# The last store of a row-wise maximum-norm kernel, cut into two halves on two queues

## Chip, cores and metric

The kernel runs on one NeuronCore of one Trainium2 chip. The metric is the device time of one execution in microseconds (us), lower being better. Before the change three runs took 626.57, 627.03 and 627.04 us; the median is 627.03 us.

## What is computed

The input is an 8192 x 8192 matrix of float32, 268.44 MB. For each row the largest absolute value is wanted, so the output is 8192 float32 numbers, 32 KB.

```python
def setup_inputs():
    return {"x": np.random.randn(8192, 8192).astype(np.float32)}

def reference(x):
    return np.linalg.norm(x, ord=np.inf, axis=1)
```

## The kernel before

Each of the 128 partitions takes whole rows. The rows are divided in two groups. The first 6144 rows, the bulk, are loaded by 24 DMAs (line 303), each bringing two rows, that is 16384 numbers, to every partition; one VectorE instruction per load (`absmax`, line 296) reduces both rows and writes two results into `r_bulk`. The last 2048 rows, the tail, are 16 rows per partition. They are loaded in smaller and smaller pieces (lines 315 and 341, 20 and 12 DMAs), so that VectorE has little left to reduce when the last piece arrives. Partial maxima go to `part` and to spare columns of `t`, and the 16 results of each partition end up in `r_tail`, a tile of 128 x 16. All 56 loads are issued by SyncE (SP), in program order, on its own queue.

Two stores write the output. ScalarE (ACT), which computes nothing here, issues the store of `r_bulk` on its queue (line 357): 128 partitions x 4 pieces of 48 bytes, 24 KB. It is held back until the third last reduction has run. SP issues the store of `r_tail` (line 359): 128 partitions x 64 bytes, 8 KB, contiguous in the output. It needs the last two reductions, one for each of the two rows that end last.

A DMA raises a semaphore when it has landed, by one for each of the 16 DMA engines. The tile framework deals eight such semaphores, called DMAHW0 to DMAHW7, to the DMAs in turn, and it makes a DMA wait for the previous user of its semaphore. The store of `r_bulk` has DMAHW0 (number 100 in the trace), the store of `r_tail` DMAHW1 (101). VectorE counts its finished reductions on semaphore 102.

The end of the program is written by hand in `finish_on_pool` (lines 89 to 140). After the body every engine reports at a barrier (semaphore 96) that GpSimd (POOL) collects and releases (97). Then POOL alone has to see that the stores have landed, and to set the semaphores back to zero for the next execution. The function finds the last DMA of SP and calls its semaphore the lane; it sorts the waits that are still open into the lane's own and the others, and builds this sequence for POOL:

```python
    last = [s for s in waits if s.id == lane]
    others = [s for s in waits if s.id != lane]
...
    tail = [wait([s], []) for s in others]
    for a, b in ((lo, lane - 1), (lane + 1, hi)):
        if a <= b:
            tail.append(clear_range(nc, clear, a, b))
...
    tail.append(wait(last, [reset]))
```

So POOL waits for the other stores, clears all semaphores below the lane, clears all above it, and last waits for the lane and subtracts its count. In the kernel before the lane is DMAHW1 and the others are DMAHW0 alone, so the end of POOL's program is: wait for the store of `r_bulk`, clear 99 to 100, clear 102 to 108, wait for the store of `r_tail` and reset 101.

`drop_implied_waits` (line 152) removes waits of SP's DMAs that another wait already implies; it does not touch DMAs of ACT. The remaining functions at the end of the kernel move the first load and a clearing instruction forward and take VectorE out of the opening barrier.

In the built program all 58 DMAs, loads and stores, move 128 partitions, and the builder has put the mark `ant_dge_precooked: true` on each of them.

Of the kernel before, what the change touches and what calls it, by code (L numbers as in the profile page):

```python
# [38 lines left out]
def segments(loads, cols):  # L39

    out, at = [], 0
    for i, w in enumerate(loads):
        end = at + w
        while at < end:
            r = at // cols
            to = min(end, (r + 1) * cols)
            out.append((i, r, at - r * cols, to - at))
            at = to
    return out
# [201 lines left out]
@with_exitstack  # L251
def kernel(
    ctx: ExitStack,
    tc: tile.TileContext,
    x: bass.AP,
    out: bass.AP,
    G: int = 6,
    B: int = 2,
    BUFS: int = 3,
    PAD: int = 256,  # L260
    LINE: int = 128,
):
    nc = tc.nc
    P = nc.NUM_PARTITIONS
    rows, cols = x.shape
    W = B * cols


    n_tail = B * (len(TAIL) + 1)
    n_bulk_rows = rows // P - n_tail  # L270
    assert n_bulk_rows % (G * B) == 0
    A = n_bulk_rows // (G * B)
    split = n_bulk_rows * P
    x_b = x[:split].rearrange("(a p n b) c -> a n p (b c)", p=P, a=A, n=G, b=B)
    out_b = out[:split].rearrange("(a p n b) -> p a (n b)", p=P, a=A, n=G, b=B)
    x_t = x[split:].rearrange("(p t b) c -> t p (b c)", p=P, b=B)
    out_t = out[split:].rearrange("(p t) -> p t", p=P)

    outp = ctx.enter_context(tc.tile_pool(name="outp", bufs=1))
    sbuf = ctx.enter_context(tc.tile_pool(name="sbuf", bufs=BUFS))  # L280

    segs = [segments(loads, cols) for loads in TAIL]
    k_max = max(sum(r == b for _, r, _, _ in s) for s in segs for b in range(B))
    parts_of = [sum(r == b for r, _ in LAST) - 1 for b in range(B)]
    assert sum(parts_of) <= PAD

    r_bulk = outp.tile([P, A, G * B], F32)
    r_tail = outp.tile([P, n_tail], F32)
    part = outp.tile([P, n_tail - B, k_max], F32)
    used = [HEAD, A * G * B, n_tail, (n_tail - B) * k_max]  # L290
    gap = -sum(-(-n // STEP) * STEP for n in used) % LINE
    outp.tile([P, gap], F32, name="gap")
    nc.gpsimd.memset(part[:], 0.0)  # L293

    def absmax(o, i):
        return nc.vector.reduce_max(  # L296
            out=o, in_=i, axis=X, apply_absolute_value=True
        )

    for a in range(A):  # L300
        for n in range(G):
            t = sbuf.tile([P, W + PAD], F32, tag="t")
            nc.sync.dma_start(out=t[:, :W], in_=x_b[a, n])
            absmax(
                r_bulk[:, a, n * B : (n + 1) * B],
                t[:, :W].rearrange("p (b c) -> p b c", b=B),
            )

    for i, loads in enumerate(TAIL):
        t = sbuf.tile([P, W + PAD], F32, tag="t")  # L310
        todo = segs[i]
        seen = [0] * B
        at = 0
        for j, w in enumerate(loads):
            nc.sync.dma_start(out=t[:, at : at + w], in_=x_t[i][:, at : at + w])
            at += w
            for _, b, c, n in [s for s in todo if s[0] == j]:
                k, lo = seen[b], b * cols + c
                absmax(part[:, i * B + b, k : k + 1], t[:, lo : lo + n])
                seen[b] += 1  # L320

    def after(ins, first, kind):
        info = mybir.DependencyInfo(kind, mybir.DependencyReason.SCHED_ONLY)
        tc.add_manual_dep(ins.ins, first.ins.name, info, reason="order")


    t = sbuf.tile([P, W + PAD], F32, tag="t")
    left = parts_of[:]
    col = [0] * B
    at, slot = 0, {}  # L330
    ends = [w for _, w in LAST[-B:]]
    lo = W - sum(ends)
    for b in range(B):
        slot[b] = -(-lo // LINE) * LINE + ends[b]
        lo = slot[b] + parts_of[b]
    assert lo <= W + PAD
    for j, (b, w) in enumerate(LAST):
        final = left[b] == 0
        to = slot[b] - w if final else at
        frm = b * cols + col[b]  # L340
        nc.sync.dma_start(out=t[:, to : to + w], in_=x_t[len(TAIL)][:, frm : frm + w])
        col[b] += w
        if final:
            r = n_tail - B + b
            absmax(r_tail[:, r : r + 1], t[:, to : slot[b] + parts_of[b]])
        else:
            left[b] -= 1
            k = slot[b] + left[b]
            done = absmax(t[:, k : k + 1], t[:, to : to + w])
            at += w  # L350
        if j == 0:

            ins = absmax(r_tail[:, : n_tail - B], part[:])
            after(ins, done, mybir.DependencyClass.NoSync)
        if j == len(LAST) - 3:

            ins = nc.scalar.dma_start(out=out_b, in_=r_bulk[:])
            after(ins, done, mybir.DependencyClass.Sync)
    nc.sync.dma_start(out=out_t, in_=r_tail[:])
    nc.at_finalize(clear_partials_early)  # L360
    nc.at_finalize(drop_implied_waits)
    nc.at_finalize(start_first_load_early)
    nc.at_finalize(finish_on_pool)
    nc.at_finalize(open_without_vector)
# [30 lines left out]
```

## Time and profile before

| what | value | where it is read |
|---|---|---|
| median of three runs | 627.03 us | the runs |
| span of the profiled execution, first to last instruction | 624.1 us (624.05) | head of the page |
| VectorE busy | 552.4 us, 89% of the span | part 1 |
| DMA traffic | 268.47 MB, mean 430 GB/s | part 2 |
| packets of the load queue q1 | 8064 in the span, 99.7% of 16 engines' time | part 3 |

The page gives no total for the profiled execution besides its span. What lies around the span is 627.03 - 624.05 = 2.98 us if that execution took as long as the median.

The span ends with the last instruction of the program, but the last store is still under way then. The trace also records the semaphores being raised, and it goes on after the span. Its events around the end, in us from the span's start, are these; duration is that of the instruction.

| us | event |
|---|---|
| 621.57 | VectorE's count that releases the store of `r_bulk` |
| 621.59 | ACT issues the store of `r_bulk`, 0.409 |
| 622.04 | ACT's drain before the barrier, 0.153 |
| 622.54 to 623.13 | 512 data packets and 16 semaphore packets of that store on the DMA engines |
| 623.275 to 624.000 | its 16 landings (semaphore 100) |
| 623.297 | VectorE's last count, which releases the store of `r_tail` |
| 623.314 | SP issues the store of `r_tail`, 0.348 |
| 623.720 | SP's drain, 0.123; SP is the last at the barrier, 623.845 |
| 623.947 | POOL's release of the barrier; seen on semaphore 97 at 623.972 |
| 624.065 | POOL clears 99 and 100 |
| 624.138 to 624.166 | POOL clears 102 to 108 |
| 624.157 to 624.37 | 128 data packets and 16 semaphore packets of the store of `r_tail` |
| 624.565 to 624.730 | its 16 landings (semaphore 101) |
| 624.780 | POOL's reset of 101, its last act in the program |
| 624.29, 624.32, then 625.33 to 625.62 | counts on semaphore 2, the runtime's own, after the program |
| 625.52 to 626.22 | the runtime clears all other semaphores |
| 626.45 to 626.80 | a last round of counts on semaphore 2 |

### The profile page before, as it was taken

How to read it: one execution, taken by the hardware profiler on the slowest of the kernel's cores; microseconds unless marked ns; L12 is line 12 of the kernel's file. 1: busy time of each engine (PE TensorE's matmuls, PEld its weight loads, DVE VectorE, ACT ScalarE, POOL GpSimd, SP SyncE). 2: the span in 40 equal slices, each digit the busy share in tenths (PEclk: the TensorE clock that was granted, in tenths of full speed). 3: DMA queues.
4: the chain of work that ended last, by engine and by line, in shares of the span. 5: the costliest groups of instructions: out<-in, count | busy, mean ns of one | idle time of the engine just before them, and what ended most of it. 6: DMA issues, size and time to landing. Idle time of an engine off the chain costs nothing.

```text
span 624.1 us, 151 instructions
## 1 busy us (share of the span) xinstructions
DVE 552.4 (89%) x63; POOL 0.3 (0%) x5
## 2 busy tenths in 40 slices
DVE  0688988889988899888898888988889999999999
POOL 0000000000000000000000000000000000000000
DMA  9999999999999999999999999999999999999998
GB/s 403 470 403 454 420 428 445 403 470 403 470 403 441 433 403 470 403 470 403 470 403 470 403 462 412 437 437 403 470 434 397 440 448 422 422 437 430 429 427 354
DMA packets 8593, 268.47 MB, mean 430 GB/s; under 512 B 1424, under 2 KB 1424, under 8 KB 2832
## 3 DMA queue, kind: packets, MB, share of 16 engines
q1 hardware_dynamic: 8064, 268.44, 99.7%
q10 hardware_dynamic: 528, 0.02, 0.1%
q14 instruction: 1, 0.01, 0.0%
HBM read 268.44 MB, written 0.03 MB: 430 GB/s over the span
## 4 chain that ended last, share of the span: by engine, by line
DMA 63%; DVE 36%; another core or an unknown queue 0%; DVEq 0%; issue 0%
DMA t<-in_x_dram 63%; DVE r_bulk L296 25%; DVE part L296 8%; DVE t L296 3%; DVEq L390 0%; DVE r_tail L296 0%
## 5 line engine op out<-in xcount | busy, mean ns | idle before, releaser
L296 DVE TENSOR_REDUCE r_bulk<-t 128x2 f32<-128x16384 f32 x24 | 413.3, 17220 | 70.6 <-DMA t<-in_x_dram 70.6
L296 DVE TENSOR_REDUCE part<-t 128x1 f32<-128x8192 f32 (+19 forms) x26 | 121.3, 4741 | 0.3
L296 DVE TENSOR_REDUCE t<-t 128x1 f32<-128x1792 f32 (+7 forms) x10 | 16.3, 1692 | 0.0
L296 DVE TENSOR_REDUCE r_tail<-t 128x1 f32<-128x772 f32 (+1 forms) x2 | 1.8, 948 | 0.0
L296 DVE TENSOR_REDUCE r_tail<-part 128x14 f32<-128x42 f32 x1 | 0.2, 192 | 0.0
L293 POOL MEMSET part<- 128x42 f32 x1 | 0.1, 133 | 0.0
L379 POOL MEMSET const-bfloat16-1.0<- 128x1 bf16 x1 | 0.1, 101 | 0.0
L379 POOL MEMSET const-uint8-127<- 128x1 uint8 x1 | 0.1, 101 | 0.0
L379 POOL MEMSET const-float32-0.0<- 128x1 f32 x1 | 0.1, 98 | 0.2 <-issue 0.2
L379 POOL MEMSET const-float32-1.0<- 128x1 f32 x1 | 0.1, 98 | 0.0
## 6 DMA issues: line engine op xcount, KB each, us to landing
t<-in_x_dram SPq DMA_DIRECT2D x2, 4672.0 KB, 37.5
t<-in_x_dram SPq DMA_DIRECT2D x2, 3520.0 KB, 36.2
t<-in_x_dram SPq DMA_DIRECT2D x1, 6336.0 KB, 36.3
t<-in_x_dram SPq DMA_DIRECT2D x1, 5696.0 KB, 40.5
t<-in_x_dram SPq DMA_DIRECT2D x2, 1792.0 KB, 34.3
t<-in_x_dram SPq DMA_DIRECT2D x1, 3392.0 KB, 37.5
t<-in_x_dram SPq DMA_DIRECT2D x1, 3008.0 KB, 44.2
t<-in_x_dram SPq DMA_DIRECT2D x1, 2496.0 KB, 27.3
```

The lines of the kernel that those rows point to most:

```text
L293: nc.gpsimd.memset(part[:], 0.0)
L296: return nc.vector.reduce_max(out=o, in_=i, axis=X, apply_absolute_value=True)
L379: nc = _bacc.Bacc("TRN2", target_bir_lowering=False, num_devices=1)
```

## The change

The store of `r_tail` is replaced by two stores of 64 partitions each. ACT issues the one of partitions 64 to 127, SP the one of partitions 0 to 63. The destination of each is a contiguous 4 KB of the output.

```diff
             ins = nc.scalar.dma_start(out=out_b, in_=r_bulk[:])
             after(ins, done, mybir.DependencyClass.Sync)
-    nc.sync.dma_start(out=out_t, in_=r_tail[:])
+    half = P // 2
+    nc.scalar.dma_start(out=out_t[half:], in_=r_tail[half:, :])
+    nc.sync.dma_start(out=out_t[:half], in_=r_tail[:half, :])
     nc.at_finalize(clear_partials_early)
     nc.at_finalize(drop_implied_waits)
```

`finish_on_pool` is unchanged, but it is given one store more. In the built program ACT's half takes DMAHW1 and SP's half DMAHW2 (103 in the trace), so that the lane is now DMAHW2 and the others are DMAHW0 and DMAHW1. ACT's program gets two instructions: a wait for the load that used DMAHW1 before, and the DMA, which waits for VectorE's last count. The instructions of the other engines are the same up to the end block, where POOL has one wait more. Neither half carries the mark `ant_dge_precooked`.

```
POOL, end block, before                   after
                                          wait DMAHW1 >= 128   (ACT's half)
clear 99..100   [wait DMAHW0 >= 128]      clear 99..102   [wait DMAHW0 >= 128]
clear 102..108                            clear 104..108
wait DMAHW1 >= 128, subtract 128          wait DMAHW2 >= 128, subtract 128
```

## The prediction, made before the changed kernel was run

> **What bounds the kernel now.** I read the page's head first, then the chain of waits, then the last microseconds by timeline, DMA view and SP's waits. The head and the chain's summary say where the 624 us are:
>
> ```profile
> span 624.1 us, 151 instructions
> DVE 552.4 (89%) x63; POOL 0.3 (0%) x5
> DMA 63%; DVE 36%; another core or an unknown queue 0%; DVEq 0%; issue 0%
> ```
>
> The chain consists of loads and of the reductions that follow them, and the change touches neither: all loads stay in SP's queue ahead of the store, with their waits, their tiles and their order. So I take 621 of the 624 us as fixed, and only what follows the last reduction is in play. The last pieces of the chain of waits (start, length, what):
>
> ```profile
> 607.80 13.50 DVE t L296 x9
> 621.30 0.17 issue
> 621.47 0.76 DVE r_tail L296
> 622.24 0.09 issue
> 622.32 0.96 DVEq L390
> ```
>
> The chain ends with VectorE at 623.28. The timeline from 619 us on shows what is issued after it:
>
> ```profile
> 621.47 1.81 DVE L296 TENSOR_REDUCE r_tail<-t 128x1 f32<-128x772 f32 x2
> 621.59 0.41 ACTq L357 DMA_DIRECT2D out_dram<-r_bulk  x1
> 623.31 0.35 SPq L359 DMA_DIRECT2D out_dram<-r_tail  x1
> ```
>
> ACT issues the bulk store 1.72 us before SP issues the last one, and is then free: its drain is over at 622.19. In SP's own waits the last store waits on VectorE and on nothing else, so SP is not a bottleneck there:
>
> ```profile
> SPq L359 <- DVE r_tail L296: 11.6, 1, 11.6
> ```
>
> The DMA view of the stretch 620 to 626 us (40 slices of 0.15 us, tenths busy) shows both stores, and the issue rows give the time from issue to last landing:
>
> ```profile
> DMA  9999999999310000187500000001400000000000
> q10 hardware_dynamic: 528, 0.02, 5.6%
> out_dram<-r_bulk ACTq DMA_DIRECT2D x1, 24.0 KB, 2.4
> out_dram<-r_tail SPq DMA_DIRECT2D x1, 8.0 KB, 1.4
> ```
>
> What the reader is to see: the last store occupies the engines for little more than one slice (the "14"), yet needs 1.4 us. By the events listed with the profile, 0.843 us pass from issue to the first packet (623.314 to 624.157), about 0.21 us are packets (to 624.37), and the last landing comes at 624.730. Data movement is the smallest share, and it is the only one that halving can shrink. POOL closes the program at 624.780, 0.050 us after that landing: the store is on the path that sets the program's end, while POOL's two clears (624.065 to 624.166) are over 0.4 us earlier and cost nothing.
>
> **The change, part by part.**
>
> *Fewer packets per store.* Each half has 64 data packets of 64 bytes instead of 128, four per DMA engine instead of eight; successive packets of one engine stand about 10 ns apart, so a half is over 4 x 10 ns = 0.04 us sooner. But both halves share the 16 engines. If they arrive together the second gains nothing. So -0.04 us for a half that runs alone, 0 if they collide; I take -0.04. The Trainium skill, in "DMA: Bandwidth & Descriptors", section "Issuing engines are not separate DMA queues", says that DMAs of several engines run on the same 16 DMA engines and that issuing them from several only saves the sequencer's time. By that rule the gain here would be 0 rather than 0.04, as no second issue is saved; the sum moves by 0.04 us.
>
> *The issue itself.* Every issue in this trace is of a marked DMA: the loads' take 0.327 to 0.433 us, the last store 0.348, the four-piece bulk store with 512 packets 0.409. The number of packets hardly matters: (0.409 - 0.348)/384 is 0.16 ns for each, so 64 fewer save 0.01 us, and I exclude a larger gain. The halves carry no mark, and no row has an unmarked issue. If the mark means preparation at build time, then the sequencer does that work now, at the worst place, because nothing follows VectorE's last count except the store. Low end: no change, 0.348. High end: the issue grows to the whole 0.843 us that now pass from issue to first packet, +0.50. No row is nearer to one end, so I take the middle, +0.25 (an issue of 0.60 us), for each half. Packets and landing move with it. SP's half: last landing 624.73 + 0.25 - 0.04 = 624.94.
>
> *ACT's half.* It waits for DMAHW1 of a load finished before 616 us, at no cost, and then for VectorE's last count, like SP. ACT has nothing behind the DMA but its drain. Its start reaction is the same (0.021 us after the count for the bulk store, 0.017 for SP's). From its issue to its first packet the bulk store took 622.540 - 621.589 = 0.951 us against SP's 0.843, so ACT's way is 0.11 us longer (0.06 of it the longer issue, which its four-piece shape may explain). I take +0.08, ends 0.05 and 0.11. ACT's half therefore lands at 624.94 + 0.08 = 625.02.
>
> *The barrier.* SP reaches it at 623.845 today, ACT at 622.20. With the longer issue SP comes at 624.09, and ACT, with 0.05 us more for its drain (0.153 plus 0.04 gap), at about 624.2. The release moves from 623.97 to 624.3, still 0.7 us before the landings, which hide it.
>
> *POOL's end.* Here work loses its cover. POOL now waits for ACT's landing first, then clears twice, then waits for SP's half. So the two clears, which today run under the flight of the store, stand behind a landing. From rows of the same instructions: wait satisfied to its end 0.05 (624.730 to 624.780), next the first clear 0.093 (from the release's count at 623.972 to 624.065), the second clear 0.073 after it and 0.028 long, the last wait's reset another 0.05: 0.29 us after ACT's landing. Before it was 0.05. So +0.24 if ACT's half lands last or together with SP's; if it lands more than 0.24 us before SP's it costs nothing. I take it whole, as ACT's is the later one.
>
> *Sum.* 625.02 + 0.29 = 625.31 for POOL's last act, against 624.78: +0.53 us (0.25 issue, 0.08 ACT's way, 0.24 clears, -0.04 packets). Lowest by these bounds: no longer issue, +0.05 for ACT: 0 + 0.05 + 0.24 - 0.04 = +0.25. Highest: 0.50 + 0.11 + 0.24 + 0 = +0.85. The span itself, which ends at the last instruction with a record, should grow as well.
>
> From program to time: POOL's last act is at 624.78, the runtime's last recorded count at 626.80, and I let the 2.02 us between stay. The profiled execution's total is not given; span 624.05 plus 2.98 us around it is the median, 627.03. So I forecast **627.03 + 0.53 = 627.56, rounded 627.6 us**. A measurement of this kernel tells about 0.2% from no change, 1.25 us: the forecast is slower by 0.08% and counts as no change.
>
> **The rivals.**
>
> *The halves are issued one after the other (chance 0.17).* Then the change does not do what it says. Both are released by one count, and SP reacts 4 ns sooner, so ACT's would be second, by one issue more: 0.35 to 0.60 us. It carries POOL's clears along: 625.31 + 0.35 to 0.60 gives +0.88 to +1.13 us, 627.9 to 628.2. For it: nothing in the trace excludes it. Against it: nothing shows it either, as ACT's one issue at 621.59 meets no issue of SP, whose last load was issued by 611.7 (573.31 plus 38.40 in SP's timeline). The Trainium skill, in "Perfetto Trace Analysis", section "DMA Instruction — HWDGE (DVE, Sync)", describes one descriptor generator that sequencers lock for exclusive use, with the lock's wait inside the profiled issue; by that rule the second issue would be the longer record. No run here shows it yet.
>
> *ACT's half lands as slowly as the bulk store did (0.15): slower.* ACT's queue has one sample, 2.41 us from issue to last landing against SP's 1.42. If this belongs to the queue and not to the 512 packets of 48 bytes, ACT's half lands at 623.32 + 2.41 = 625.73, with the longer issue 625.98, and POOL ends 0.29 later, 626.27: +1.49 us, 628.5. It counts as slower once ACT's landing comes later than 624.78 + 1.25 - 0.29 = 625.74, that is 2.42 us after the issue. Against it: of the 2.41 us, 0.59 are packets, and the landings trail the last packet by 0.87 us where the 64-byte store has 0.36; both go with the many small writes.
>
> *The end is covered (0.14).* The runtime's counts come at 624.29 and 624.32, and then not before 625.33, 0.55 us after POOL's reset. If these wait for something other than POOL, say another engine that starts its closing code when the barrier is released, only the barrier's delay of 0.3 us or less is felt: 627.0 to 627.3.
>
> *The gain arrives (0.06).* The issue is no longer, ACT's half lands 0.24 us or more before SP's, and a half is 0.04 us sooner: 627.0, at best 626.9. A gain over 1.25 us is not to be had, since the whole way from VectorE's last count to POOL's reset is 624.78 - 623.30 = 1.48 us and holds an issue, a start and a landing in any case.
>
> **How the numbers follow.** My forecast holds 0.48. Of it 0.06 may run over 1.25 us, if the longer issue exceeds its bound or the runtime's closing round is delayed too. Slower: 0.15 + 0.06 + 0.05 (the worst of the issues in turn with an issue of 0.84 us) = 0.26. Faster: only by scatter of the runs, 0.02. Same: 0.72. The range goes from 627.0 (covered end) to 628.6 (the slow landing, 0.1 above its value).
>
> **What would show it.** Right: the issue record of each half is about 0.6 us instead of 0.35; both start within 0.02 us of VectorE's last count; ACT's landings end about 0.1 us after SP's; POOL's clears stand behind ACT's last landing and its reset of 103 comes near 625.3; everything up to 623.3 is as before. Wrong: one issue record nearly twice as long as the other (in turn); ACT's landing 2.4 us after its issue; the clears still at 624.1; or a POOL end 0.5 us later with the total unmoved. A time below 626.6 would mean that I have missed a wait which the second queue removes; one above 628.7 that a part of the program I took as fixed has moved.

## The result and the profile after

The changed kernel took 627.33 us (median of 21 runs, 627.10 to 627.62) against 626.56 us for the kernel before in 21 runs of the same sessions (626.33 to 627.04). The ratio is 1.0013, with a 95% interval of 1.0007 to 1.0018. That is 0.8 us slower: clear of no effect by its interval, and inside the 0.2% that the prediction called no change. Against this larger sample the first three runs of the kernel before (median 627.03) were on the high side.

The head of the page of the changed kernel and the summary of its chain of waits:

```profile
span 624.8 us, 153 instructions
DVE 552.4 (88%) x63; POOL 0.3 (0%) x5
DMA 63%; DVE 36%; another core or an unknown queue 0%; DVEq 0%; issue 0%
```

VectorE's work is the same to 0.1 us. The span is 0.7 us longer. The last pieces of its chain of waits (start, length, what):

```profile
607.81 13.51 DVE t L296 x9
621.32 0.18 issue
621.50 0.76 DVE r_tail L296
622.25 0.08 issue
622.33 0.98 DVEq L392
```

Each stands within 0.03 us of where it stood before, so the loss lies behind VectorE's last count. The timeline there (start, length, engine, line, what):

```profile
621.50 1.81 DVE L296 TENSOR_REDUCE r_tail<-t 128x1 f32<-128x772 f32 x2
621.61 0.43 ACTq L357 DMA_DIRECT2D out_dram<-r_bulk  x1
623.34 0.53 SPq L361 DMA_DIRECT2D out_dram<-r_tail  x1
623.34 0.54 ACTq L360 DMA_DIRECT2D out_dram<-r_tail  x1
```

Both halves are issued at once, and both issues are half as long again as the whole store's 0.35. The DMA view of 620 to 626 us (tenths busy in slices of 0.15 us; below it size and time from issue to last landing):

```profile
DMA  9999999998520000257610000000002020000000
out_dram<-r_tail SPq DMA_DIRECT2D x1, 4.0 KB, 1.7
out_dram<-r_tail ACTq DMA_DIRECT2D x1, 4.0 KB, 2.0
```

Where the view of before had one "14", there are now two separate "2"s, with a slice below a tenth between them and both later than the "14". The halves leave SP and ACT at the same time, but they do not travel at the same time, and each needs longer than the whole store did (1.4).

The semaphore events and the packet records of the two traces, in us after VectorE's last count, give the account:

| us after VectorE's last count | before | after | difference |
|---|---|---|---|
| SP's store: first packet | 0.860 | 1.188 | +0.328 |
| SP's store: last landing | 1.433 | 1.708 | +0.275 |
| ACT's store: first packet | | 1.457 | |
| ACT's store: last landing | | 1.981 | 0.273 after SP's |
| POOL's last act | 1.483 | 2.284 | +0.801 |
| from the last landing to POOL's last act | 0.050 | 0.303 | +0.253 |
| from POOL's last act to the runtime's next count | 0.553 | 0.553 | 0 |

The sum 0.275 + 0.273 + 0.253 is 0.801 us, and the times differ by 0.77. The experiments ask what makes each of the three terms.

### The profile page after: what moved, and what is told of

It reads as the page before. It is cut to its first block, busy times and chain, and to the rows that moved or that the text cites. A ratio compares the mean times of both kernels' runs of the same rounds, so it can differ in the third digit from the quotient of the medians.

```text
span 624.8 us, 153 instructions
## 1 busy us (share of the span) xinstructions
DVE 552.4 (88%) x63; POOL 0.3 (0%) x5
## 4 chain that ended last, share of the span: by engine, by line
DMA 63%; DVE 36%; another core or an unknown queue 0%; DVEq 0%; issue 0%
DMA t<-in_x_dram 63%; DVE r_bulk L296 25%; DVE part L296 8%; DVE t L296 3%; DVEq L392 0%; DVE r_tail L296 0%
```

## The experiments

All positions below are us after VectorE's last count, from the semaphore events and the packet records of each trace, unless they are said to be after the issue. Each position is from one profiled execution of its kernel. The drain is the last instruction that an engine runs before it is counted at the barrier.

**The mark alone: the whole store on SP, built without it**

`dge_precook` is the builder's switch for the mark; it is off for this one store.

```diff
+    nc.dge_precook = False
     nc.sync.dma_start(out=out_t, in_=r_tail[:])
+    nc.dge_precook = True
```

> The kernel before, with its one store of 128 partitions on SyncE's queue, but that store is built without the mark ant_dge_precooked. Theory (the missing mark makes the issue longer, whatever the number of queues and partitions): the issue record is about 0.53 us instead of 0.348, the first packet comes about 1.17 us after the issue instead of 0.843, the last landing about 1.7 us after the issue instead of 1.42, and POOL's last act moves from 624.78 by 0.28 to 0.33 us; the time is 0.3 us above the kernel before (ratio 1.0004 to 1.0006). Rival (the longer issue came from two queues issuing at once): issue 0.35, first packet 0.84, landing 1.42, ratio 1.0000. Second rival (it came from the 64-partition shape): the same as the first here, but the SyncE half alone shows 0.53.

The rows of the last store in this kernel, one from the view by tile (issue in ns, three times the same, and when), one from the DMA view:

```profile
L360 SPq DMA_DIRECT2D out_dram<-r_tail x1: 542/542/542, 623.1 to 623.1; - x1
```
```profile
out_dram<-r_tail SPq DMA_DIRECT2D x1, 8.0 KB, 1.8
```

One queue and 128 partitions, as before, and the issue is 0.542 us instead of 0.348. The first packet comes at 1.202 (1.185 after the issue), the last landing at 1.781, POOL's last act at 1.830: +0.347 us, slightly more than expected. The time was 627.02 against 626.66 us, ratio 1.0005 (0.9996 to 1.0014). The interval alone would not settle it, the trace does: the mark is worth 0.35 us, and neither the second queue nor the number of partitions is needed for that.

**ScalarE's queue alone: the whole marked store on ACT**

```diff
-        if i.engine == sp and type(i).__name__ == "InstDMACopy"
+        if type(i).__name__ == "InstDMACopy"
...
-    nc.sync.dma_start(out=out_t, in_=r_tail[:])
+    nc.scalar.dma_start(out=out_t, in_=r_tail[:])
```

> The kernel before, with its one marked store of 128 partitions issued by ScalarE instead of SyncE, and POOL's last wait on that store. Theory (ScalarE's queue is itself only about 0.1 us slower): issue 0.35 to 0.41, first packet 0.95 after the issue, last landing 1.5 to 1.55 us after it, time 0.1 us above the kernel before (ratio 1.0002). Rival (ScalarE's queue is slow by nature, as the bulk store's 2.41 us to landing suggested): landing 1.7 us or more after the issue, up to 2.4, time 0.3 to 1.0 us above (ratio 1.0005 to 1.0016).

```profile
L359 ACTq DMA_DIRECT2D out_dram<-r_tail x1: 351/351/351, 623.0 to 623.0; - x1
```
```profile
out_dram<-r_bulk ACTq DMA_DIRECT2D x1, 24.0 KB, 2.4
out_dram<-r_tail ACTq DMA_DIRECT2D x1, 8.0 KB, 1.4
```

The issue (view by tile, above) and the landing (DMA view, below it) are those of SP: first packet 0.874 against 0.860, POOL's last act 1.491 against 1.483, time 626.65 against 626.66 us, ratio 1.0001 (0.9992 to 1.0010). Both the expected 0.1 us and the rival fall. On the same queue, 1.7 us apart, the bulk store needs 2.4 us and the tail store 1.4: it is the store that is slow, not the queue.

**Each half alone**

Each of these two kernels leaves one half out, so that half of the tail's output is not written. Each was executed once (627.08 and 626.97 us), and only the positions in their traces are used.

```diff
     nc.scalar.dma_start(out=out_t[half:], in_=r_tail[half:, :])
-    nc.sync.dma_start(out=out_t[:half], in_=r_tail[:half, :])
```

> ScalarE's half alone: the store of partitions 0 to 63 is left out, so half of the tail's output is not written; POOL's last wait is on ScalarE's half. It asks why ScalarE's half ran 0.27 us behind SyncE's in the changed kernel. If the two halves' descriptors were made one after the other, it is faster without the other: drain 0.36 us or less instead of 0.632, first packet 1.17 to 1.28 us after the issue instead of 1.436, last landing 1.7 to 1.8 us after the issue instead of 1.96. If ScalarE's queue is slower by nature: drain 0.63, first packet 1.44, landing 1.96 as in the changed kernel.

```diff
-    nc.scalar.dma_start(out=out_t[half:], in_=r_tail[half:, :])
     nc.sync.dma_start(out=out_t[:half], in_=r_tail[:half, :])
```

> SyncE's half alone: the store of partitions 64 to 127 is left out, so half of the tail's output is not written. Theory (the mark alone, SyncE went first and was not held up): as in the changed kernel, issue 0.526, drain 0.36, first packet 1.17 us after the issue, last landing 1.69. Rival (two queues hold each other up): issue 0.35, first packet 0.84, last landing 1.38 to 1.42.

The issue of ACT's half alone and, in the second fence, that of SP's half alone, from the view by tile:

```profile
L360 ACTq DMA_DIRECT2D out_dram<-r_tail x1: 513/513/513, 623.4 to 623.4; - x1
```
```profile
L360 SPq DMA_DIRECT2D out_dram<-r_tail x1: 525/525/525, 623.3 to 623.3; - x1
```

| | first packet | last landing | engine's drain |
|---|---|---|---|
| SP's half alone | 1.188 | 1.714 | 0.360 |
| SP's half in the changed kernel | 1.188 | 1.708 | 0.359 |
| ACT's half alone | 1.192 | 1.724 | 0.398 |
| ACT's half in the changed kernel | 1.457 | 1.981 | 0.632 |

SP's half does not notice the other. ACT's half alone is as quick as SP's; beside SP's it comes 0.257 us later. So the delay is a turn that it waits for: ACT's store was issued 5 ns after SP's. The other order was not tried. The wait is hardly in the issue's record (0.542 against 0.513); it is in ACT's drain, which lasts 0.234 us longer. Without the other half the drain was 0.398 where 0.36 or less was expected, which changes nothing. A half by itself is 0.067 us quicker to land than the unmarked whole (1.714 against 1.781): that is what the smaller store is worth, and 0.033 of it is the shorter time of its packets (0.180 against 0.213).

**POOL's clears ahead of both waits**

```diff
-    tail = [wait([s], []) for s in others]
-    for a, b in ((lo, lane - 1), (lane + 1, hi)):
...
-    tail.append(wait(last, [reset]))
+    late = {
+        i.sync_info.on_update[0].id
+        for i in [i for i in body.instructions if type(i).__name__ == "InstDMACopy"][-2:]
+    }
+    tail = [wait([s], []) for s in others if s.id not in late]
+    a = lo
+    for b in sorted(late) + [hi + 1]:
+        if a < b:
+            tail.append(clear_range(nc, clear, a, b - 1))
+        a = b + 1
+    for s in [s for s in waits if s.id in late]:
+        reset = mybir.SyncUpdate(
...
+        tail.append(wait([s], [reset]))
```

> The changed kernel with one thing undone: POOL clears 99 to 100, 102 and 104 to 108 while the halves are under way, and waits for both halves last, resetting 101 and 103 one after the other. Theory (the two clears behind ScalarE's landing cost 0.25 us of the changed kernel's 0.80): POOL's last act comes 0.05 to 0.10 us after the last landing instead of 0.303, 2.03 to 2.08 us after VectorE's last count instead of 2.284; the time is 0.2 to 0.25 us below the changed kernel, 0.55 to 0.6 above the kernel before (ratio 1.0009). Rival (the end is covered by something other than POOL): POOL ends sooner, the runtime's counts and the time stay, ratio 1.0013.

The stores land as in the changed kernel (1.723 and 1.974), the three clears run at 1.46 to 1.63 under their flight, POOL resets 101 at 2.023, 0.049 after the landing, and 103 at 2.119. That is later than the expected 2.03 to 2.08, which left out the second reset, 0.096 us. From the last landing to POOL's last act it is now 0.145 us, so 0.158 of the 0.253 us came back. The time was 627.24 us, 0.59 above the kernel before, ratio 1.0010 (1.0001 to 1.0019); the runtime's next count again followed 0.553 us after POOL. So nothing else covers the end.

**Halves that keep the mark, cut by columns**

```diff
-            absmax(r_tail[:, r : r + 1], t[:, to : slot[b] + parts_of[b]])
+            fin = absmax(r_tail[:, r : r + 1], t[:, to : slot[b] + parts_of[b]])
...
-    nc.scalar.dma_start(out=out_t[half:], in_=r_tail[half:, :])
-    nc.sync.dma_start(out=out_t[:half], in_=r_tail[:half, :])
+    n = n_tail // 2
+    ins = nc.scalar.dma_start(out=out_t[:, n:], in_=r_tail[:, n:])
+    after(ins, fin, mybir.DependencyClass.Sync)
+    ins = nc.sync.dma_start(out=out_t[:, :n], in_=r_tail[:, :n])
+    after(ins, fin, mybir.DependencyClass.Sync)
```

> The two halves are cut by columns instead of partitions: each store has 128 partitions x 8 numbers (32 bytes), so both carry the mark; both wait for VectorE's last count, ScalarE stores columns 8 to 15 and SyncE columns 0 to 7; POOL's sequence is that of the changed kernel. Theory of terms (the missing mark 0.35, in turn 0.26, clears 0.25, fewer packets -0.06): the mark's 0.35 goes away, issues are about 0.35 us and SyncE's first packet comes 0.86 us after VectorE's last count. If the halves are made in turn whatever their mark, ScalarE's packets start 0.2 to 0.26 us after SyncE's and POOL's last act is 1.9 to 2.0 us after VectorE's last count (ratio 1.0007). If the turn belongs to the unmarked way of issuing, both start together and POOL ends at about 1.73 us (ratio 1.0004). If pieces of 32 bytes land more slowly, the time from last packet to last landing exceeds 0.38 us; that is seen apart.

The issues (view by tile) and the DMA view of 620 to 626 us of this kernel:

```profile
L363 SPq DMA_DIRECT2D out_dram<-r_tail x1: 343/343/343, 623.3 to 623.3; - x1
L361 ACTq DMA_DIRECT2D out_dram<-r_tail x1: 383/383/383, 623.3 to 623.3; - x1
```
```profile
DMA  9999999999320000277500000000810000000000
out_dram<-r_tail SPq DMA_DIRECT2D x1, 4.0 KB, 1.4
out_dram<-r_tail ACTq DMA_DIRECT2D x1, 4.0 KB, 1.6
```

Both bursts now fall into one spot, the "81": first packets at 0.853 (SP) and 0.907 (ACT). The mark is there again, the long issue is gone, and the turn has shrunk from 0.27 to 0.05 us. POOL ended at 1.892, close to the 1.9 to 2.0 expected for halves in turn, but for another reason: ACT's half landed at 1.588, 0.162 after SP's, since its last landing trails the end of its packets by 0.48 us where SP's trails by 0.37. The time was 627.08 us, ratio 1.0007 (0.9998 to 1.0015). SP's half, with half the bytes in as many packets, landed at 1.426; the whole store of before landed at 1.433.

The same halves with POOL's clears first, that is this diff and the one before together:

> The column halves with the mark, and POOL's clears ahead of both waits: all three costs that can be undone are undone, and only the turn is left. Theory: POOL's last act 0.05 to 0.10 us after the last landing, 1.5 to 1.75 us after VectorE's last count against 1.483 in the kernel before; time 0 to 0.27 us above the kernel before (ratio 1.0000 to 1.0004). A time below the kernel before would mean that two queues do save something; by the theory they cannot, because packets were never more than 0.2 us of the store's way.

Landings at 1.432 and 1.595, POOL's resets at 1.644 and 1.740. Time 626.92 us, 0.27 above the kernel before, ratio 1.0004 (0.9996 to 1.0013). This is the best form of the idea that was tried. By the trace it still ends 0.257 us later than the kernel before: 0.16 because the second half lands later, 0.10 for the second reset.

**Both halves on SP**

```diff
-    nc.scalar.dma_start(out=out_t[half:], in_=r_tail[half:, :])
+    nc.sync.dma_start(out=out_t[half:], in_=r_tail[half:, :])
     nc.sync.dma_start(out=out_t[:half], in_=r_tail[:half, :])
```

> Both 64-partition halves on SyncE's queue, partitions 64 to 127 first; POOL's sequence is that of the changed kernel (wait for the first half, clear, wait for the second). Theory (a generator that serves one store at a time): the second half costs one whole issue more, 0.5 to 0.6 us, so its last landing comes 2.2 to 2.35 us after VectorE's last count, and POOL's last act 0.05 after that, its clears being hidden under the second half: 2.25 to 2.4 us, about as in the changed kernel (2.284); ratio to the kernel before 1.0012 to 1.0015. Rival (queueing on one engine is far worse than two queues): 2.6 us or more, ratio 1.0018 or more.

The two issues, from the view by tile:

```profile
L360 SPq DMA_DIRECT2D out_dram<-r_tail x1: 526/526/526, 623.2 to 623.2; - x1
L361 SPq DMA_DIRECT2D out_dram<-r_tail x1: 586/586/586, 623.8 to 623.8; - x1
```

The second half starts 0.57 us after the first, lands at 2.351 and POOL ends at 2.400: 627.51 us, ratio 1.0015 (1.0006 to 1.0024). Two queues bring the second landing 0.37 us forward against one, but POOL's clears, which here hide under the second half, eat most of it (2.284 against 2.400). The Trainium skill says in "DMA: Bandwidth & Descriptors", section "Issuing engines are not separate DMA queues", that issuing from several engines only saves the sequencer's time; the 0.37 us saved here, less than one issue record of 0.586, agree with it.

**What the turn belongs to: column halves without the mark, and with one mark**

The first edit is shown against the column halves above.

```diff
     n = n_tail // 2
+    nc.dge_precook = False
     ins = nc.scalar.dma_start(out=out_t[:, n:], in_=r_tail[:, n:])
     after(ins, fin, mybir.DependencyClass.Sync)
     ins = nc.sync.dma_start(out=out_t[:, :n], in_=r_tail[:, :n])
+    nc.dge_precook = True
```

> The column halves (128 partitions x 8 numbers each) with the mark taken from both; POOL's sequence is that of the changed kernel. In the changed kernel ScalarE's first packet came 0.27 us after SyncE's, with the marked column halves 0.054 us. Theory (the turn belongs to the unmarked way of issuing, not to the cut by partitions): ScalarE's first packet 0.25 to 0.3 us after SyncE's (1.46 against 1.19 us after VectorE's last count), its drain 0.6 us instead of 0.15, POOL's last act about 2.35 us after that count. Rival (it belongs to the cut: 64 partitions on each queue): first packets 0.05 us apart, POOL at about 2.15 us.

For the second kernel the first added line stands before SP's store instead, so that ACT's keeps its mark.

> The column halves, ScalarE's with the mark, SyncE's without. Theory (an unmarked issue holds something that another unmarked issue needs, and a marked one passes it early): ScalarE's packets start about 0.87 to 0.91 us after VectorE's last count, SyncE's at 1.19 to 1.25; SyncE's half lands last, at 1.75 to 1.8, POOL's clears are hidden under it, and POOL ends at 1.8 to 1.85 us. Rival (one generator in order of arrival, SyncE being first): ScalarE's packets wait for SyncE's and start at 1.2 us or later, and POOL ends at 2.1 us or later.

| | ACT's first packet | SP's first packet | ACT's drain | POOL's last act |
|---|---|---|---|---|
| both marked | 0.907 | 0.853 | 0.152 | 1.892 |
| ACT's marked, SP's not | 0.873 | 1.199 | 0.153 | 1.825 |
| neither marked | 1.468 | 1.200 | 0.650 | 2.344 |
| changed kernel (64 partitions, neither marked) | 1.457 | 1.188 | 0.632 | 2.284 |

The issues in the view by tile, of the kernel without marks and, in the second fence, of the kernel with one mark:

```profile
L364 SPq DMA_DIRECT2D out_dram<-r_tail x1: 540/540/540, 623.3 to 623.3; - x1
L362 ACTq DMA_DIRECT2D out_dram<-r_tail x1: 539/539/539, 623.3 to 623.3; - x1
```
```profile
L364 SPq DMA_DIRECT2D out_dram<-r_tail x1: 541/541/541, 623.0 to 623.0; - x1
L361 ACTq DMA_DIRECT2D out_dram<-r_tail x1: 352/352/352, 623.0 to 623.0; - x1
```

Without marks the column halves behave like the halves by partitions. A marked store passes an unmarked one that was issued 5 ns earlier, and neither is held up: their first packets come at 0.873 and 1.199, where the whole stores, each without a neighbour, had 0.874 (marked, on ACT) and 1.202 (unmarked, on SP). So the 0.26 us turn appears only between two unmarked issues; it is neither the cut nor an order of arrival. A marked store issued ahead of an unmarked one was not tried. Each of these two kernels was executed once, so they rest on their traces; their times, 627.50 and 626.76 us against 626.57, are 0.93 and 0.19 us longer where POOL's positions give 0.86 and 0.34, and single executions of the kernel before lie up to 0.7 us apart.

**POOL's last act against the time.** For every kernel that was executed more than once, the shift of POOL's last act agrees with the shift of the time to within 0.06 us:

| | POOL's last act, minus 1.483 | median, minus that of before |
|---|---|---|
| whole store on ACT | +0.008 | -0.01 |
| marked halves, clears first | +0.257 | +0.27 |
| whole store without mark | +0.347 | +0.36 |
| marked halves | +0.409 | +0.43 |
| halves, clears first | +0.636 | +0.59 |
| changed kernel | +0.801 | +0.77 |
| both halves on SP | +0.917 | +0.86 |

## Why the prediction held, and where it did not

The forecast was +0.53 us, no change by the 0.2% bound; the trace has +0.80. Time, range and direction held. That the time, 627.56 against 627.33 us, came so near is partly luck: the start of 627.03 was 0.47 above the later median of the kernel before, and the sum was low. By the trace it was low by 0.27 us, and one of its terms rested on a mechanism that the runs refute.

*Fewer packets, -0.04.* Right: a half is worth 0.067 us, by the half alone against the unmarked whole, and the packets of the two halves did not meet in the changed kernel.

*The issue, +0.25, between 0 and 0.50.* Right in kind, a little small: 0.347 us by the mark alone. Of that 0.194 stand in the issue's record (0.542 where about 0.60 was forecast); the rest lies between the record's end and the first packet. The middle between two far ends was a guess; only the list of DMAs in the built program showed that the halves are of another kind, and no row of the profile of before could.

*ACT's half, +0.08.* This is the step that failed. The prediction took ACT's queue to be slower by itself, from one sample: "From its issue to its first packet the bulk store took 622.540 - 621.589 = 0.951 us against SP's 0.843". The queue is not slower: the whole store on ACT's queue ended 0.008 us later than on SP's. The sample's 0.11 us belonged to the bulk store. What delays ACT's half is the turn, 0.257 us by ACT's half alone, which the prediction had only as a rival; in the changed kernel ACT's half landed 0.273 us after SP's.

*The barrier, hidden.* Right, with less room than thought: the drains behind unmarked stores are longer (0.36 and 0.63 us where 0.123 and 0.153 were read before), ACT's lasts until 624.557, so the release comes at 624.693 instead of the forecast 624.3; SP's last landing follows at 625.030.

*POOL's clears, +0.24.* Right: 0.253. Two of its parts missed in opposite ways: the first clear ends 0.110 us after ACT's last landing where 0.143 was added up, and the last reset takes 0.096 instead of 0.05. Taking the clears out of the way gives back only 0.158, because the second store then needs a reset of its own, 0.096 us.

*The rivals.* "The halves are issued one after the other" named the right mechanism and missed its size and the place where it shows in the trace: 0.26 us instead of 0.35 to 0.60, and in the drain, not in an issue record "nearly twice as long as the other". The Trainium skill ("Perfetto Trace Analysis", section "DMA Instruction — HWDGE (DVE, Sync)") describes a lock for exclusive use, and the turn of two unmarked issues, 0.27 us between their first packets, agrees with that; that the lock's wait lies inside the profiled issue does not agree with 0.542 against 0.513 us here. Two marked issues have their first packets 0.05 us apart. "ACT's half lands as slowly as the bulk store did" falls: 1.42 us from issue to landing for the whole store on ACT's queue. "The end is covered" falls: the runtime's next count follows POOL's last act by 0.553 or 0.554 us in every trace. "The gain arrives" falls, the best form still ending 0.257 us late.

## What to carry to other kernels

The small store at the end of this program is nearly all fixed cost: 0.2 of 1.43 us are packets. An unmarked half was 0.07 us quicker than the unmarked whole at best, while the second store added a wait to POOL's end and, where it was reset by itself, 0.096 us. Before cutting a DMA, compare the built instructions of the whole and of the parts: a part can fall into a slower class of issue, as the halves did here, and the profile of before cannot show it. And a hand-written end sequence must be told of every late store: one that knows of a single last store puts its remaining work behind the other one.

## What the runs showed of the hardware beyond that

- The mark `ant_dge_precooked` is worth 0.19 us in the issue's record (0.542 against 0.348) and 0.34 us to the first packet (1.202 against 0.860), on a store of the same shape and queue.
- Two unmarked issues on SP and ACT at the same time take turns, 0.27 us between their first packets. With two marked ones it is 0.05 us, and the marked one did not wait for an unmarked one (first packets at 0.873 and 1.199).
- A store that waits for its turn shows it in the drain that follows on its engine (0.63 against 0.40 us) and hardly in its own record (0.542 against 0.513).
- Where both marked halves arrived together, ACT's last landing came 0.11 us later after the end of its packets than SP's (0.48 against 0.37), in both such traces. In the two other column kernels, whose halves share the same 64-byte pieces of the output but travel 0.06 us or more apart, both queues need 0.36 to 0.37. So the shared pieces alone do not do this; the two bursts have to meet. Whether meeting bursts do it without shared pieces was not tried and stays open.
